# Value products of twelve heads in groups of four, sixteen places for transposed probabilities, one compressed transpose per four heads, and an end in token halves, in a two-layer decoder trunk

## The chip, the cores and the metric

The kernel runs on one core of one Trainium2 chip. The metric is the device time of one execution in microseconds (us). Three runs of the kernel before gave 577.61, 577.78 and 578.94 us, so the median is 577.78 us. The engines are named PE (TensorE, matrix products), PEld (its weight loads), DVE (VectorE), ACT (ScalarE), POOL (GpSimd) and SP (SyncE, which issues most transfers).

## The reference, cut to what matters

The trunk has two layers for 256 tokens of width 1024. Layer 0 is a recurrent block (gates, short convolution, scan) with a squared-ReLU MLP. Layer 1 is sparse attention with the same kind of MLP. A final norm ends it. With 256 tokens, a window of 512 and four selected blocks out of four, the selected and the window branch both see all earlier keys.

```python
x = x + _rglru_mixer(_rmsnorm(x, norm_mix[0]), ...);  x = x + _sq_relu_mlp(_rmsnorm(x, norm_ffn[0]), ...)
x = x + _nsa_mixer(_rmsnorm(x, norm_mix[1]), ...);    x = x + _sq_relu_mlp(_rmsnorm(x, norm_ffn[1]), ...)
return _rmsnorm(x, norm_final)
# in the attention, 16 heads in 4 groups that share keys and values:
o = g[..., 0:1] * o_c + g[..., 1:2] * o_s + g[..., 2:3] * o_w   # compressed, selected, window
```

The compressed branch has 15 keys: windows of 32 tokens at a stride of 16, each put through a small MLP. o_c, o_s and o_w are softmax(scores) times values, in each branch.

## The kernel before

All activations lie transposed: channels on the 128 partitions, 256 tokens along the free dimension, in 8 chunks. A weight comes in pieces of 128x1024 (load from L254), and ACT or DVE splits it into a high and a low part (L268, L277, or L316, L313 in the planned sections). mm3 (L307 to L310) makes each product of three matmuls of 128x256: high by high, high by low, low by high.

Two sections, the recurrent block (from 0 to about 62 us) and the attention (about 270 to 400 us), are written as lists of tasks with engine, length, due time and keys that they read or write. The class Plan turns such a list into one fixed order for every engine: it adds a random number up to SHIFT = 1.5 to each due time, from a seed (SEEDS = (11, 19), one for each section), lists, improves six times, and emits. Between and behind these sections run the two MLPs (function mlp), in an order written out by hand.

In the attention the steps that matter here are:
- hidden and vc_out make the 15 compressed values of each group. vc_out copies them to hv, multiplies by w2raw in four products of 64 columns (L944) and spreads them into bd, whose rows 64 to 127 are set to zero by POOL (L947 is the spreading).
- compressed(a) makes the compressed scores of four heads in bank 7, eleven steps on DVE and ACT make probabilities of them (cq: 128 query tokens by two token halves x 4 heads x 16 keys), two transposes (L1052), one for each token half, put them in bank 7, and ACT copies them (L1054) to pc: 64 partitions, 256 tokens.
- scores(s), rescale(s), transposes(s), for head s of 16: the scores of both other branches (L1075, L1076), the softmax (L1082, L1085), its scaling (L1104, L1105), and six transposes (L1116) with two copies into pT (L316). pT has 8 places of 128x384, two to a head.
- pv(j), j from 0 to 7, for two heads: the value products (L1127) into bank 7, two at a time for the two halves of the output partitions. A pair over pc and bd with 256 columns comes first, then for each branch a pair with 256 and a pair with 128 columns. All are float32, which is two matmul instructions each, so pv has 20. Then ACT or DVE copies the bank to oh (L316) and DVE makes the rest ol (L313).
- qchunk, kchunk and out_t: the projections before and behind, which fill PE between heads.

In the last MLP, m = 7 ends with: add to the residual (L508), square (L473), sums of squares over the partitions (L500), root (L1215) and reciprocal, spreading over the partitions (L505), six multiplications (L1220), and a transfer out of each (L1221).

Of the kernel before, what the change touches and what calls it, by code (L numbers as in the profile page):

```python
# [12 lines left out]
F32 = mybir.dt.float32  # L13
# [21 lines left out]
SEEDS, ROUNDS, SHIFT = (11, 19), 6, 1.5  # L35
# [184 lines left out]
def trunk_kernel(ctx: ExitStack, tc: tile.TileContext, x_in, vec_in, const_in, w2_in, wts, out):  # L220
# [524 lines left out]
    def mlp(layer, epilogue, first, late=None):  # L745
        with ExitStack() as ph:
            up = ph.enter_context(tc.tile_pool(name="up%d" % layer, bufs=1, side="right"))
            tmp = ph.enter_context(tc.tile_pool(name="mtmp%d" % layer, bufs=2))
            uhl = [up.tile([P, 2 * S], F32R, name="uhl", tag="uhl", bufs=NF) for _ in range(NF)]
# [24 lines left out]
            for m in range(8):  # L774
                z = next(zrot)[:, :S]
                for j in range(4):
                    if j == 3 and late and m == 7:
                        late()
                    wh, wl = get("dn%d" % layer, m * 4 + j)
                    for k in range(8):  # L780
                        w, i = slice(k * P, (k + 1) * P), j * 8 + k
                        mm3(z, wh[:, w], wl[:, w], uh[i], ul[i], i == 0, i == NF - 1)
                    if j == 3:
                        residual(z, m)
                        epilogue(m)
                    tick()
# [8 lines left out]
    with ExitStack() as ph:  # L795
# [9 lines left out]
        bd = at.tile([P, 4, 4, 64], F32, name="bd")  # L805
# [13 lines left out]
        pTt = at.tile([P, 8, 3 * P], F32, name="pT")  # L819
        pT = [pTt[:, i] for i in range(8)]  # L820
        w1 = many([P, 1024], F32, "w1", 2)
        pcs = many([P, S], F32, "pc", 2)
        for i in range(2):
            o = offs[-1] + (4 + i) * P * 1024
            add("sp", 1.5, lambda e, i=i, o=o: e.dma_start(w1[i], wts[o:o + P * 1024].rearrange("(p n) -> p n", p=P)),
                w=[("w1", i), "loads"], t=-12, lag=2.0)
        add("pool", 1.74, lambda e: e.memset(kl.bitcast(F32), 0.0), w=["kl"], t=-9)
        add("pool", 0.15, lambda e: e.memset(kc.bitcast(F32), 0.0), w=["kc0"], t=-9)
        add("pool", 0.9, lambda e: e.memset(bd[64:], 0.0), w=["bd0"], t=-8)
        for i in range(2):  # L830
            add("pool", 0.3, lambda e, i=i: e.memset(pcs[i][64:], 0.0), w=[("pc0", i)], t=-8)
# [52 lines left out]
        hid = pre.tile([P, 4, NCP], F32, name="hid")  # L884
        hv = pre.tile([P, 4, 2, 2, NCP], F32, name="hv")[64:]
        hvs = hid[64:]
        add("pool", 0.15, lambda e: e.memset(hid, 0.0), w=["hid"], t=-5)
# [19 lines left out]
        def hidden(b, t):  # L907
# [3 lines left out]
            for q_ in range(4):  # L911
# [4 lines left out]
                add("pe", 0.86, run, r=[("w1", i) for i in range(2)] + keys + zpt, w=[("ps", b)], t=t + 0.9 * q_)  # L916
# [4 lines left out]
                r=[("ps", b), "cb", "tab"], w=["hid"], t=t)  # L921

        def kc_out(t):
            o = zview("kco", 6, lambda x: x[:, :4 * NCP])
            add("pe", 0.3, lambda e: e.matmul(o(), w2raw[:64], hid[:64].rearrange("p g n -> p (g n)"), start=True, stop=True),
                r=["hid"], w=[("ps", 6)], t=t)
# [8 lines left out]
        def vc_out(t):  # L935
            for g in range(4):
                dst = hv[:, g // 2 * 2:g // 2 * 2 + 2, :, g % 2].rearrange("p a b n -> p (a b) n")
                add([("act", 0.2, 0.0), ("dve", 0.15, 0.0)], copy(dst, hvs[:, g, None, :].to_broadcast([64, 4, NCP])),
                    r=["hid"], w=[("hv", g)], t=t)
            o = zview("vco", 7, lambda x: x[:64, :4 * 64].rearrange("p (a e) -> p a e", a=4))  # L940
# [4 lines left out]
            add("pe", 0.9, run, r=[("hv", g) for g in range(4)], w=[("ps", 7)], t=t)  # L945
            for a in range(4):
                add("dve", 0.34, lambda e, a=a: e.tensor_tensor(  # L947
                    bd[:64, a], o()[:, a, None, :].to_broadcast([64, 4, 64]),
                    cst[:64, C_BM:C_BM + 4, None].to_broadcast([64, 4, 64]), op=OP.mult), r=[("ps", 7)], w=[("bd", a)], t=t)
# [47 lines left out]
        css, cs2, cmx = many([P, 4, 2, NCP], F32, "cs", 2), many([P, 2, 4, NCP], F32, "cq", 2), many([P, 8], F32, "cm", 2)  # L997
# [4 lines left out]
        def compressed(a, t, dt):  # L1002
# [39 lines left out]
            for i, (d, fn, r, w) in enumerate(steps):  # L1042
                if d == "act":
                    add("act", 0.2, fn, r=r, w=w, t=t + dt * i)
                else:
                    add("dve", d, fn, r=r, w=w, t=t + dt * i)
            t += dt * len(steps)
            ct_ = zview(("ct", a), 7, lambda x: x[:64, :S])

            def tr(e):  # L1050
                for qc in range(2):
                    e.transpose(ct_()[:, qc * P:(qc + 1) * P], sq_[:, qc].rearrange("p j n -> p (j n)"), identf)  # L1052
            add("pe", 0.22, tr, r=[qk], w=b7, t=t)
            add("act", 0.26, lambda e: e.copy(pc[:64], ct_()), r=b7, w=[pk], t=t)  # L1054
# [53 lines left out]
        def transposes(s, t):  # L1108
            pt = pts[s % NPT]
            for b in range(2):  # L1110
# [7 lines left out]
                i = s // 2 % 2 * 4 + s % 2 * 2 + b  # L1118
                add([("act", 0.38, 0.0), ("dve", 0.47, 0.2)], lambda e, tp=tp, i=i: copy(pT[i], tp())(e), r=bk, w=[("pT", i)], t=t + 0.3)

        def pv(j, t):
            p, a, n0 = j // 4, j // 2, j % 2 * 4
            bk = [("ps", 7)]
            o = zview(("o", j), 7, lambda x: x[:, :S])

            def run(e):
                two = lambda c0, w, y, **k: [e.matmul(o()[own_(hf), c0:], w(hf), y(hf), **k) for hf in range(2)]  # L1127
                two(0, lambda hf: bd[:, a, j % 2 * 2 + hf], lambda hf: pcs[a % 2], start=True, stop=False)
                for b in range(2):
                    y = lambda hf: pT[n0 + 2 * hf + b]  # L1130
                    two(0, lambda hf: vv[:, 0, b, 2 * p + hf], lambda hf: y(hf)[:, :S], start=False, stop=False)
                    two(P, lambda hf: vv[:, 1, b, 2 * p + hf], lambda hf: y(hf)[:, S:], start=False, stop=b == 1)
# [197 lines left out]
```

## Time and profile before

| | us |
|---|---|
| median of three runs | 577.78 |
| the profiled execution, its own time | 578.3 |
| its span in the trace | 576.5 |
| PE busy in the span | 564.8 |
| PE busy from 302 to 382 us (heads) | 79.81 of 80 |
| DVE busy there | 75.78 of 80 |
| from the start of the last addition to the residual to the end of the span | 9.4 |

The span is what the trace covers; the profiled execution's own time has 1.8 us more around it. "Busy" counts an engine as working while an instruction is under way. PE's instructions overlap: one of 256 columns is shown with 0.28 us and the next starts 0.11 us later. So what an instruction costs in a full stream is read from start to start. The page's TensorE clock is full in all but the last of 40 slices.

### The profile page before, as it was taken

What the parts mean: (1) busy time and instruction counts of PE and PEld (TensorE: products, weight loads), DVE (VectorE), ACT (ScalarE), POOL (GpSimd) and SP (SyncE); (2) the same over time, 40 slices, a digit from 0 to 9 for tenths busy, and PEclk for the clock granted to TensorE, in tenths of its full rate; (3) what the DMA queues carried; (4) which work ended last, traced back from release to release, by engine and by line L of the source; (5) the groups of instructions that cost most, each with busy time, mean ns of one, the idle gap of its engine ahead of it and who ended that gap; (6) DMA issues with size and microseconds to landing.
All of it is one profiled execution on the core that took longest, in us unless ns stands there. A gap on an engine that the chain in (4) does not pass through costs nothing.

```text
span 576.5 us, 12291 instructions
## 1 busy us (share of the span) xinstructions
PE 564.8 (98%) x4866; PEld 552.6 (96%) x4866; DVE 411.8 (71%) x841; ACT 338.6 (59%) x656; POOL 47.0 (8%) x60
## 2 busy tenths in 40 slices
PE   8999999999999999999999999999999999999994
PEld 7999999999999999999999888989999999999994
DVE  6899999766775664665759999978876775553522
ACT  7699585865663533444457989865766564443400
POOL 1210000000000211312000000000000000222310
PEclk9999999999999999999999999999999999999998
DMA  8934566766666566466573243243666667467302
GB/s 291 395 115 147 187 221 195 211 211 185 195 204 221 161 209 215 155 207 241 186 261 121 70 124 127 100 118 137 190 204 194 189 197 237 155 207 223 113 1 73
DMA packets 32378, 103.66 MB, mean 180 GB/s; under 512 B 4017, under 2 KB 7217, under 8 KB 32321
## 3 DMA queue, kind: packets, MB, share of 16 engines
q1 hardware_dynamic: 31712, 102.29, 54.9%
q8 instruction: 38, 0.62, 0.4%
q10 hardware_dynamic: 576, 0.53, 0.3%
q14 instruction: 20, 0.16, 0.1%
q0 software_dynamic: 32, 0.07, 0.0%
HBM read 99.23 MB, written 1.05 MB: 174 GB/s over the span
## 4 chain that ended last, share of the span: by engine, by line
PE 87%; DVE 7%; DMA 2%; ACT 1%; issue 1%; SPq 0%; DVEq 0%
PE bank L308 26%; PE bank L310 25%; PE bank L309 25%; PE bank L1127 3%; PE bank L1116 2%; DVE wlo L313 2%; DVE xb L645 2%; DMA raw<-in_dram 1%; PE bank L1075 1%; DMA xt<-in_dram 1%; PE bank L1076 1%; PE bank L965 1%; PE bank L966 1%; PE bank L967 1%; PE bank L915 1%
## 5 line engine op out<-in xcount | busy, mean ns | idle before, releaser
L308 PE MATMUL bank<-hhl,whi 128*128 128x256 f32 x768 | 214.3, 279 | 1.1 <-DVE whi L316 0.6
L310 PE MATMUL bank<-hhl,wlo 128*128 128x256 f32 x768 | 212.6, 277 | 0.8 <-DVE wlo L313 0.8
L309 PE MATMUL bank<-hhl,whi 128*128 128x256 f32 x768 | 212.6, 277 | 0.1
L308 PEld LDWEIGHTS bank<-hhl,whi 128*128 128x128 f32 x768 | 144.2, 188 | 1.9 <-ACT x L562 0.8
L310 PEld LDWEIGHTS bank<-hhl,wlo 128*128 128x128 f32 x768 | 144.2, 188 | 1.2 <-DVE wlo L313 1.2
L277 DVE TENSOR_TENSOR wlo<-raw,whi 128x1024 fp32r<-128x1024 f32 x115 | 143.6, 1269 | 2.3 <-ACT whi L268 2.3
L309 PEld LDWEIGHTS bank<-hhl,whi 128*128 128x128 f32 x768 | 144.2, 188 | 0.6 <-DVE hhl L558 0.3
L308 PE MATMUL bank<-uhl,whi 128*128 128x256 f32 x512 | 141.5, 276 | 0.0
L309 PE MATMUL bank<-uhl,whi 128*128 128x256 f32 x512 | 141.4, 276 | 0.0
L310 PE MATMUL bank<-uhl,wlo 128*128 128x256 f32 x512 | 141.4, 276 | 0.0
L268 ACT CAST whi<-raw 128x1024 fp32r<-128x1024 f32 x116 | 118.0, 1039 | 23.1 <-issue 18.8
L308 PEld LDWEIGHTS bank<-uhl,whi 128*128 128x128 f32 x512 | 96.1, 188 | 0.0
L310 PEld LDWEIGHTS bank<-uhl,wlo 128*128 128x128 f32 x512 | 96.1, 188 | 0.0
L309 PEld LDWEIGHTS bank<-uhl,whi 128*128 128x128 f32 x512 | 96.1, 188 | 0.0
L313 DVE TENSOR_TENSOR wlo<-raw,whi 128x1024 fp32r<-128x1024 f32 (+2 forms) x74 | 79.2, 1091 | 7.4 <-ACT whi L316 7.3
L508 DVE TENSOR_TENSOR xt<-xt,bank 128x256 f32<-128x256 f32 x40 | 16.1, 417 | 85.9 <-PE bank L310 85.8
L316 ACT CAST whi<-raw 128x1024 fp32r<-128x1024 f32 (+2 forms) x65 | 62.1, 969 | 21.9 <-DMA raw<-in_dram 7.5
L760 ACT ACTIVATE u<-t 128x256 f32<-128x256 f32 x64 | 26.7, 417 | 59.0 <-DVE t L755 59.0
L755 DVE SCALAR_TENSOR_TENSOR t<-bank,rstd 128x256 f32<-128x256 f32 x64 | 26.9, 423 | 40.8 <-PE bank L310 40.8
L1210 ACT ACTIVATE xg<-xt,vec 128x256 f32<-128x256 f32 x8 | 4.1, 511 | 48.0 <-DVE xt L508 48.0
L1085 ACT ACTIVATE pt<-pt,mx 128x128 f32<-128x128 f32 (+1 forms) x64 | 28.6, 449 | 4.2 <-DVE mx L1082 3.9
L478 POOL TENSOR_TENSOR acc<-xt 128x256 f32<-128x256 f32 x2 | 2.9, 1464 | 344.2 <-DVE xt L508 189.3
(191 smaller groups left out, 746.1 us busy)
## 6 DMA issues: line engine op xcount, KB each, us to landing
raw<-in_dram SPq DMA_DIRECT2D x173, 512.0 KB, 4.2
raw<-in_dram SPq DMA_DIRECT2D x4, 560.0 KB, 5.0
gw<-in_dram SPq DMA_DIRECT2D x4, 512.0 KB, 8.8
raw<-in_dram SPq DMA_DIRECT2D x6, 256.0 KB, 5.9
xt<-in_dram SPq DMA_DIRECT2D x4, 256.0 KB, 5.7
w<-in_dram SPq DMA_DIRECT2D x2, 512.0 KB, 6.0
kh<-kh SPq DMA_DIRECT2D x8, 64.0 KB, 2.7
kl<-tl SPq DMA_DIRECT2D x8, 64.0 KB, 2.9
```

Of the source, the lines that this page charges most:

```text
L268: (act.copy if eng is None else eng.tensor_copy)(hi_t[i % NSPL][:, :n], raw_t[i % NRAW][:, :n])
L277: (eng or dve).tensor_tensor(lo[:, :n], raw_t[i % NRAW][:, :n], hi[:, :n].bitcast(F32), op=OP.subtract)
L308: pe.matmul(ps, wh, xh, start=start, stop=False)
L309: pe.matmul(ps, wh, xl, start=False, stop=False)
L310: pe.matmul(ps, wl, xh, start=False, stop=stop)
L313: return lambda e: e.tensor_tensor(o, a, h.bitcast(F32), op=OP.subtract)
L316: return lambda e: (e.copy if e is act else e.tensor_copy)(o, a)
L508: dve.tensor_tensor(xt[:, m], xt[:, m], z, op=OP.add)
L755: dve.scalar_tensor_tensor(t, z, 0.0, rs, op0=OP.max, op1=OP.mult)
L760: act.activation(u, t, AF.Square)
L1085: add("act", (0.39, 0.49)[qc], lambda e, row=row, j=j: e.activation(row, row, AF.Exp, bias=mx[:, j:j + 1], scale=-1.0, accum_out=sm[:, j:j ...
L1127: two = lambda c0, w, y, **k: [e.matmul(o()[own_(hf), c0:], w(hf), y(hf), **k) for hf in range(2)]
```

## The change

Five things change.
- The value products are made for js = (0, 1), (2, 3), (4, 5), (6,), (7,): three times a run of 48 instructions for four heads, into all 512 columns of bank 7, and twice a run of 24 for two heads. The due time is that of the last member. One copy and one remainder follow each run, over 512 or 256 columns.
- pT has 16 places. The two pieces w1 of hidden lie in places 8 to 13 in place of tiles of their own, with keys that keep them apart.
- The probabilities of the compressed branch are transposed once for four heads, both token halves together (128 partitions, 128 tokens). bd holds masked values for both halves, and the pair over pc and bd becomes two pairs of 128 columns. vc_out has two products with 128 columns of weights in place of four with 64, and two wider spreadings in place of four; the settings to zero go.
- hid, hv, and the scores and probabilities of the compressed branch lie in the tiles sq0 and sq1, which the norms use, with keys for that.
- The end: PE adds the old residual of the last chunk into its bank at the start of m = 7 (two matmuls with the identity). ACT then squares the bank directly, by token halves; sums, root, reciprocal and spreading are made for each half in banks of their own, then once more into banks 0 and 1 for a copy in SBUF, and five multiplications and transfers follow, the first two of 3 chunks by half the tokens.

The seeds of both planned sections are others, too: (3, 0) for (11, 19).

```diff
-SEEDS, ROUNDS, SHIFT = (11, 19), 6, 1.5
+SEEDS, ROUNDS, SHIFT = (3, 0), 6, 1.5
...
+                if last and m == 6:
+                    act.copy(ir, ident)
+                    act.copy(xh, xt[:, 7])
+                    diff(xl, xt[:, 7], xh)(dve)
+                if seeded:
+                    pe.matmul(z, ir, xh, start=True, stop=False)
+                    pe.matmul(z, ir, xl, start=False, stop=False)
...
-        pTt = at.tile([P, 8, 3 * P], F32, name="pT")
-        w1 = many([P, 1024], F32, "w1", 2)
-        pcs = many([P, S], F32, "pc", 2)
+        NPT_ = 16
+        pTt = at.tile([P, NPT_ * 3 * P], F32, name="pT")
+        w1 = [pTt[:, 8 * 3 * P + i * 1024:8 * 3 * P + (i + 1) * 1024] for i in range(2)]
+        w1k = [("pT", i) for i in range(8, 14)]
+        pcs = many([P, P], F32, "pc", 2)
...
-                for a in range(4):
-                    e.matmul(o()[:, a], hv[:, a].rearrange("p b f n -> p (b f n)"), w2raw[64:, :64], start=True, stop=True)
+                for p in range(2):
+                    e.matmul(o()[:, p], hv[:, p].rearrange("p b f n -> p (b f n)"), w2raw[64:, :64], start=True, stop=True)
...
-                for qc in range(2):
-                    e.transpose(ct_()[:, qc * P:(qc + 1) * P], sq_[:, qc].rearrange("p j n -> p (j n)"), identf)
-            add("act", 0.26, lambda e: e.copy(pc[:64], ct_()), r=b7, w=[pk], t=t)
+            add("pe", 0.11, lambda e: e.transpose(ct_(), sq_.rearrange("p q j n -> p (q j n)"), identf), r=[qk, ("sq", 1)], w=b7, t=t)
+            add([("act", 0.3, 0.0), ("dve", 0.2, 0.15)], lambda e: copy(pc, ct_())(e), r=b7, w=[pk], t=t)
...
+                    for qc in range(2):
+                        two(tok[qc], lambda hf: bd[:, p, qc * 4 + j % 2 * 2 + hf], lambda hf: pcs[a % 2], start=qc == 0,
+                            stop=False)
...
-        for j in range(8):
-            events.append((T0 + (2 * j + 3.4) * T, 1, lambda j=j: pv(j, T0 + (2 * j + 3.4) * T)))
+        for js in ((0, 1), (2, 3), (4, 5), (6,), (7,)):
+            t = T0 + (2 * js[-1] + 3.4) * T
+            events.append((t, 1, lambda js=js, t=t: pv(js, t)))
...
+    def finish(z):
+        for i in range(2):
+            act.activation(sqh[i], z[:, tok[i]], AF.Square)
+        for i in range(2):
+            pe.matmul(sts[i][:, :1], sqh[i], ones, start=False, stop=True)
+        dve.tensor_scalar(xg[:, 7], z, vec[:, V_GL + 7:V_GL + 8], None, op0=OP.mult)
+        for i in range(2):
+            act.activation(rcs[i], sts[i][:, :1], AF.Sqrt, bias=epst, scale=1.0 / D)
+        for i in range(2):
+            dve.reciprocal(rcs[i], rcs[i])
+            pe.matmul(sts[i][:, S:S + P], rcs[i].to_broadcast([P, P]), ident, start=True, stop=True)
+        for i in range(2):
+            pe.matmul(dup[i][:, :P], rcs[i].to_broadcast([P, P]), ident, start=True, stop=True)
...
+    for i in range(2):
+        act.copy(rs[:, tok[i]], dup[i][:, :P])
+    for n, (a, b, i) in enumerate(((0, 3, 0), (0, 3, 1), (3, 5, 2), (5, 7, 2), (7, 8, 2))):
+        c = tok[i] if i < 2 else slice(0, S)
+        scaled(a, b, c, sts[i][:, S:S + P] if i < 2 else rs)
+        (nc.scalar if n % 2 else nc.sync).dma_start(out[:, a:b, c], xg[:, a:b, c])
```

## Rows read from the trace of the kernel before

**Rows 1.** From the page: the span, and busy time, share of the span and instructions of each engine.

```profile
span 576.5 us, 12291 instructions
PE 564.8 (98%) x4866; PEld 552.6 (96%) x4866; DVE 411.8 (71%) x841; ACT 338.6 (59%) x656; POOL 47.0 (8%) x60
```

**Rows 2.** The waits of PE over the whole span: for whom it waited, in total, how often, and the longest. The waits of the end are left out.

```profile
PE bank L310 <- DVE wlo L313: 0.8, 2, 0.7
PE bank L308 <- DVE whi L316: 0.6, 1, 0.6
PE bank L308 <- ACT hhl L556: 0.5, 1, 0.5
PE bank L1075 <- DMA sa<-tl: 0.2, 1, 0.2
```

**Rows 3.** Busy time by stretch: the recurrent section, the first MLP, the heads of the attention, the last MLP. Columns: stretch, its length, busy time and (instructions) of PE, PEld, DVE, ACT and POOL, the granted TensorE clock as a share of 2.4 GHz, the DMA share, GB/s.

```profile
0.00:65.00 65.00, 61.61 (x456) 58.91 (x457) 58.12 (x122) 50.68 (x96) 8.27 (x20) 1.00 0.62 219
65.00:180.00 115.00, 115.00 (x1014) 115.00 (x1013) 91.72 (x148) 76.14 (x132) 0.00 (x0) 1.00 0.65 207
302.00:382.00 80.00, 79.81 (x675) 71.81 (x675) 75.78 (x315) 66.38 (x208) 0.00 (x0) 1.00 0.37 112
480.00:570.00 90.00, 88.41 (x776) 87.92 (x774) 39.62 (x40) 30.40 (x37) 18.76 (x13) 1.00 0.44 140
```

**Rows 4.** The order of PE's instructions among the heads (timeline, PE alone): start, time under way, line, operation, operands, how many in a row. First a pair of compressed transposes, then a value product between transposes, then one in front of a projection.

```profile
329.57 0.38 PE L1052 MATMUL bank<-cst,cq 128*64 128x128 f32 x2
329.71 0.37 PE L308 MATMUL bank<-hhl,whi 128*128 128x256 f32 x1
...
330.50 0.49 PE L1116 MATMUL bank<-cst,pt 128*128 128x128 f32 x3
330.92 0.65 PE L1127 MATMUL bank<-pc,bd 128*64 128x256 f32 x4
331.41 1.47 PE L1127 MATMUL bank<-pT,vv 128*64 128x256 f32 x16
332.81 0.55 PE L1116 MATMUL bank<-cst,pt 128*128 128x128 f32 x3
...
334.46 0.65 PE L1127 MATMUL bank<-pc,bd 128*64 128x256 f32 x4
334.94 1.47 PE L1127 MATMUL bank<-pT,vv 128*64 128x256 f32 x16
336.34 0.39 PE L308 MATMUL bank<-hhl,whi 128*128 128x256 f32 x1
336.56 0.28 PE L309 MATMUL bank<-hhl,whi 128*128 128x256 f32 x1
```

**Rows 5.** The same view in the recurrent section: 56 float32 matmuls of 128x256 with weights of 128 columns, with nothing between, and what follows.

```profile
31.93 12.25 PE L665 MATMUL bank<-xb,gw 128*128 128x256 f32 x56
43.83 0.47 PE L308 MATMUL bank<-hhl,whi 128*128 128x256 f32 x1
```

**Rows 6.** The same view at the products of vc_out (64 columns of weights, 64 columns moved) and at the early sums of squares (128 columns of weights, one column moved), each with what follows.

```profile
286.81 0.65 PE L944 MATMUL bank<-w2raw,hv 64*64 64x64 f32 x8
287.38 0.41 PE L965 MATMUL bank<-whi,hhl 128*128 128x304 f32 x1
...
563.63 0.50 PE L500 MATMUL bank<-ones,acc 128*128 128x1 f32 x4
564.00 0.37 PE L308 MATMUL bank<-uhl,whi 128*128 128x256 f32 x1
```

**Rows 7.** Groups of instructions by line, operation and shape: count, busy time, mean ns of one, idle time before them.

```profile
L316 ACT COPY pT<-bank 128x384 f32<-128x384 f32 x30 | 13.6, 474 | 2.5 <-PE bank L1116 2.2
L316 ACT CAST oh<-bank 128x256 fp32r<-128x256 f32 x8 | 3.0, 372 | 2.6 <-PE bank L1127 2.5
L1031 ACT ACTIVATE cs<-cs 128x128 f32<-128x128 f32 x4 | 1.3, 313 | 0.4 <-DVE cs L1030 0.2
L313 DVE TENSOR_TENSOR ol<-bank,oh 128x256 fp32r<-128x256 f32 x8 | 3.3, 414 | 2.2 <-ACT oh L316 2.2
L316 DVE COPY pT<-bank 128x384 f32<-128x384 f32 x2 | 1.1, 547 | 0.0
```

**Rows 8.** The end in order of time (timeline, all engines). The first row is PE's last matmul of the last MLP.

```profile
566.82 0.28 PE L310 MATMUL bank<-uhl,wlo 128*128 128x256 f32 x1
567.13 0.42 DVE L508 TENSOR_TENSOR xt<-xt,bank 128x256 f32<-128x256 f32 x1 [11.04 <-PE bank L310]
...
567.66 0.42 DVE L473 TENSOR_TENSOR sq<-xt 128x256 f32<-128x256 f32 x1
...
568.14 0.61 PE L500 MATMUL bank<-ones,sq 128*128 128x1 f32 x4 [1.04 <-DVE sq L473]
568.78 0.26 ACT L1215 ACTIVATE rcol<-bank,epst 128x2 f32<-128x2 f32 x1 [0.68 <-PE bank L500]
569.08 0.17 DVE L1216 RECIPROCAL rcol<-rcol 128x2 f32<-128x2 f32 x1 [0.99 <-ACT rcol L1215]
...
569.29 0.71 PE L505 MATMUL bank<-cst,rcol 128*128 128x128 f32 x4 [0.55 <-DVE rcol L1216]
570.04 2.61 DVE L1220 TENSOR_TENSOR xg<-xg,bank 128x256 f32<-128x256 f32 x6 [0.80 <-PE bank L505]
```

More of the change, by code (lines that the diff above doesn't have):

```diff
@@ L743, in trunk_kernel, with mlp @@
         sec.emit(SEEDS[0])
-    def mlp(layer, epilogue, first, late=None):
+    def mlp(layer, epilogue, first, late=None, last=None):
         with ExitStack() as ph:
@@ L748, in mlp @@
             tmp = ph.enter_context(tc.tile_pool(name="mtmp%d" % layer, bufs=2))
+            if last:
+                xh, xl, ir = (tmp.tile([P, n], F32R, name=a, bufs=1) for a, n in (("xh", S), ("xl", S), ("ir", P)))
             uhl = [up.tile([P, 2 * S], F32R, name="uhl", tag="uhl", bufs=NF) for _ in range(NF)]
@@ L775, in mlp @@
                 z = next(zrot)[:, :S]
+                seeded = last is not None and m == 7
+                if last and m == 6:
[5 more added lines that the diff above has]
+                    pe.matmul(z, ir, xl, start=False, stop=False)
                 for j in range(4):
-                    if j == 3 and late and m == 7:
+                    if j == 3 and seeded:
                         late()
@@ L781, in mlp @@
                         w, i = slice(k * P, (k + 1) * P), j * 8 + k
-                        mm3(z, wh[:, w], wl[:, w], uh[i], ul[i], i == 0, i == NF - 1)
-                    if j == 3:
+                        mm3(z, wh[:, w], wl[:, w], uh[i], ul[i], i == 0 and not seeded, i == NF - 1)
+                    if j == 3 and seeded:
+                        last(z)
+                    elif j == 3:
                         residual(z, m)
@@ L804, in trunk_kernel @@
         vv = at.tile([P, 2, 2, 4, 64], F32, name="vv")
-        bd = at.tile([P, 4, 4, 64], F32, name="bd")
+        bd = at.tile([P, 2, 8, 64], F32, name="bd")
         gts = at.tile([P, 2, NH, 3], F32, name="gts")
@@ L915, in run @@
                             e.matmul(hp()[own_(i)], w1[i][:, l * 64:(l + 1) * 64], zfs[i][:, :, l], start=l == 0, stop=l == 15)
-                add("pe", 0.86, run, r=[("w1", i) for i in range(2)] + keys + zpt, w=[("ps", b)], t=t + 0.9 * q_)
+                add("pe", 0.86, run, r=[("w1", i) for i in range(2)] + keys + zpt + w1k, w=[("ps", b)], t=t + 0.9 * q_)
             t += 3.6
@@ L996, in trunk_kernel @@
         mxs, sms = many([P, 4], F32, "mx", 4), many([P, 4], F32, "sm", 4)
-        css, cs2, cmx = many([P, 4, 2, NCP], F32, "cs", 2), many([P, 2, 4, NCP], F32, "cq", 2), many([P, 8], F32, "cm", 2)
+        cmx = many([P, 8], F32, "cm", 2)
+        css = [ahf[:, i * P:(i + 1) * P].rearrange("p (j q n) -> p j q n", j=4, q=2) for i in range(2)]
+        cs2 = [alf[:, i * P:(i + 1) * P].rearrange("p (q j n) -> p q j n", q=2, j=4) for i in range(2)]
         heads = [(p, c, hf) for p in range(2) for c in range(4) for hf in range(2)]
@@ L1126, in run @@
             def run(e):
[L1127 to L1132, printed above, removed]
@@ new lines, in pv @@
+            ps = sorted({j // 4 for j in js})
+            add("pe", 1.54 * n + 0.35, run, r=[("pT", j % 4 * 4 % NPT_ + i) for j in js for i in range(4)] + [("bd", p) for p in ps] +
+                [("pc", j // 2 % 2) for j in js] + [("v", h, b) for h in range(2) for b in range(2)], w=bk, t=t)
+            ok, lk = ([(x, j) for j in js] for x in ("oh", "ol"))
+            add([("act", 0.1 + 0.24 * n, 0.0), ("dve", 0.07 + 0.27 * n, 0.2)], lambda e: copy(oht[:, cols], o())(e), r=bk, w=ok,
+                t=t + 1.9 * n)
```

88 lines of the change are left out of this document (46 added, 42 removed).

## The prediction

> **What bounds the kernel now.** I read the page first: PE is busy for 564.8 of 576.5 us, DVE for 411.8 [rows 1]. A busy PE may still be slow, so the waits come next: outside the end PE waits for 2.1 us in all, 1.9 of it for split weights and activations in the recurrent section, 0.2 for a moved query among the heads [rows 2]. Then the stretches: in the MLPs PE and PEld are both full, among the heads PE is busy for 79.81 of 80 us and DVE for 75.78 [rows 3]. Last the order of PE's instructions, since only distances from start to start tell what one costs [rows 4]. So the kernel is a chain of PE work from about 62 to 567 us, and behind it an end of 9.4 us in which the engines wait for each other [rows 8]. An edit between 270 and 400 us counts by the PE time that it takes out; what it saves on DVE and ACT counts only where PE waits for them. An edit of the end counts by its chain.
>
> **Value products.** Their own work first. The float32 matmuls of the recurrent section give a price without gaps: 56 in 43.83 - 31.93 = 11.90 us, 0.2125 us for 256 columns (the first starts beside the tail of its forerunner; I take 0.215) [rows 5]. A pair of pv runs its two halves beside each other at that price: two pairs over bd take 334.94 - 334.46 = 0.48 us, where 2 x 0.215 = 0.43 would do, and the rest (four instruction pairs of 256 and four of 128 columns, 4 x 0.215 + 4 x 0.1075 = 1.29) takes 336.34 - 334.94 = 1.40 [rows 4]. So a run pays about 0.05 at its start and 0.11 at its end. Ahead of it, three transposes take 330.92 - 330.50 = 0.42, where three at 0.11 are 0.33: another 0.09. A projection right behind pays 0.22 for its first matmul, not 0.12: 0.10 more, where no transposes stand between [rows 4]. One run thus costs 0.25 to 0.35 us beyond its work, every time that PE changes between 128-wide and 64-wide output tiles. Eight runs become five, so three such costs go: 0.75 to 1.05, and I take 0.9. The work itself stays: a pair of 256 columns becomes two of 128, whose price per column is the same inside vv (1.40 us holds both widths [rows 4]). The extra eight instructions per two heads could cost something if 128 columns didn't cover a weight load; those over vv do cover it, so I put it at nothing, with 0.2 in all as the upper end.
>
> **Compressed transposes.** Two of them take 0.14 us from the first to the projection behind, which then pays 0.2 for its first matmul [rows 4]; three transposes of full width at 0.11 show the price of one. Four of the eight go: 4 x 0.11 = 0.44 us, between 0.3 (if part of it hides in the change of the stream) and 0.44. I take 0.43.
>
> **vc_out.** The eight instructions of 64 weight columns take 287.38 - 286.81 = 0.57 us with their exit, 0.06 to 0.07 each. The early sums of squares move one column each, but load 128 columns of weights, and four take 564.00 - 563.63 = 0.37 us, 0.09 to 0.11 each [rows 6]. The new products are four instructions with 128 columns of weights: nearest to the second row, so 4 x 0.11 = 0.44 against 8 x 0.06 = 0.48, and I take no gain; the end of the range is 0.2.
> Counting instructions alone would make this half of 0.48, a gain of 0.24 us. The Trainium skill speaks against that ("TensorE: Matmul & The Clock Gate", section "LDWEIGHTS (loading the stationary operand)"): a weight load takes as long as it has columns, whatever the depth of the contraction. By that rule half as many loads of twice the width gain nothing, and the sums of squares, at about 0.1 us with one column moved, agree.
>
> **DVE, ACT, POOL.** Two copies of oh at 0.372 and two remainders at 0.414 become one of each over 512 columns [rows 7]; with the fixed part saved, 0.1 us each, three times on both engines. The zero settings on POOL go, and ACT copies 128 columns to pc in place of 256. All of this lies beside a PE that is busy, and costs or gives nothing while it stays so. The 16 places let transposes run ahead of the value products by twice as many heads; the old 8 caused no wait that PE shows [rows 2], so this is room for the grouping, not a gain. A run for four heads is one long piece of 3.7 us in PE's fixed order and waits for eight places, for pc and for bank 7. Behind it in PE's queue stand scores and projections. Due times of the last members are as before, so what out_t reads comes at the same place. w1 in places 8 to 13 is read before the first head; head 4 is the first to write there, so SP's loads and POOL's memsets get no new wait on the path. The keys on sq0 and sq1 join work that lies a stage apart.
>
> **The end.** PE first pays two more matmuls for the old residual, 0.23 us at 0.1134 each (115.00 us by 1014 in the first MLP [rows 3]); the three preparations, about 0.4 us each [rows 7], stand in ACT's and DVE's queues one chunk, some 11 us, earlier [rows 8], where ACT has 30.40 us of work in 90 and DVE 39.62 [rows 3]; PE waits for none of it. Let A be the moment at which the old addition began, 567.13, just after PE's last matmul [rows 8]. Before: addition, square, sums, root, reciprocal and spreading bring the first multiplication to 570.04, A + 2.91, and the last ends at 572.65, A + 5.52 [rows 8]. After, for the first half: square 0.31 (128 columns on ACT, rows 7), 0.06 to PE, two sums 0.38 (0.61 for four less two steps of 0.11), 0.03 and root 0.26, 0.04 and reciprocal 0.17, 0.04 and spreading 0.49 (0.71 for four less two steps), 0.04: A + 1.82. The second half follows 0.2 to 0.3 behind. DVE makes two products of 384 columns, at 2.61 us per 2048 [rows 8] 0.98 us, to A + 2.80. The other three wait for rs: second spreading to A + 2.1, two more to A + 2.5, two ACT copies of about 0.3: A + 3.1. They have 1280 columns, 1.63 us: A + 4.73. That is 0.8 sooner than A + 5.52, less 0.23 for the seed matmuls: 0.55 to 0.65. If ACT's steps overlap as DVE's do it is 0.9; if the transfers of half rows, which the trace has none of, land later, it is 0.2. I take 0.65. From the last multiplication to the span's end I keep 576.5 - 572.65 = 3.9 us.
>
> **The new seeds.** They deal all orders anew, in the recurrent section too, where nothing else changes. What that does isn't in the trace. Bounds: PE's waits there are 1.9 us, of which 0.8 are for split weights [rows 2], so the gain ends at about 0.8 there and 0.2 among the heads; a poor order can as well show those waits twice, 1.9 us more. The middle that I take is nothing.
>
> **The sum.** 0.9 + 0.43 + 0 + 0.65 = 1.98 us. The profiled execution, 578.3 us with a span of 576.5, becomes 576.3; it stands 0.5 above the median of the runs. The median of 577.78 becomes 575.8. A measurement of this kernel can tell about 0.3% from no change, which is 1.7 us: 576.05 and 579.5 are the bounds, and the forecast lies barely beyond the first.
>
> **Rivals.**
> - *PE time among the heads isn't the limit.* Taken-out work then turns into waits, and only the end's 0.65 comes: 577.1 us. For it: DVE has 4.2 us of idle in 80, and PEld is busy for 71.81 only [rows 3]. Against it: the distances from start to start are those of a full stream [rows 4, 5].
> The Trainium skill ("Trainium Kernel Development and Optimization", section "Performance Expectations") warns that matmul busy time is a bad measure and weight loads are the better one. By that rule 8.2 us of the 80 could be waits; but pairs beside each other and 512-column scores need fewer loads for the same time, so I give it little.
> - *DVE becomes the bound: slower.* Each of the 32 copies to pT is made by ACT or DVE as the plan sees fit, 30 by ACT at 0.474 and 2 by DVE at 0.547 [rows 7]. The new order may give DVE more. Its idle of 4.2 us, less 1.3 by which PE's work shrinks, plus 0.4 of saved remainders and copies, is 3.3: up to six copies moved are free, and from the seventh on each costs 0.55 us of the stage. Thirteen moved (7.1 us) make the stage 3.8 longer than forecast: 579.6 us.
> - *The new order also sheds old waits:* 0.8 in the recurrent section and 0.2 to 0.4 among the heads: 574.7 us.
> - *The grouping doesn't do what it says:* if the change of tile widths is paid at each two heads inside a run too, 0.9 goes: 576.7 us.
>
> **How the numbers follow.** Forecast 0.50, own range 574.8 to 576.9; DVE bound 0.12; PE not the limit 0.15; waits shed 0.17; cost inside runs 0.06. Faster than 576.05: 0.35 of the forecast's 0.50 and the shed waits, 0.52. Slower: 0.12. The rest, 0.36, is no change that can be told. The range runs from 574.0, the shed waits with the end's 0.9, to 578.5, which takes in PE not being the limit and a recurrent section with 1.4 us more waits; it leaves out the DVE bound and the tails.
>
> **What would show it.** Value products in five runs, with 48 instructions in about 3.6 us and no pause in the middle; four compressed transposes; PE still without waits among the heads, which then end some 1.3 us sooner; the first multiplication 1.8 us after PE's last matmul, the last at 4.7. I am wrong if PE waits for DVE or for copies among the heads, if the stretch up to 62 us changes by more than 0.5 us, or if the last transfer lands later than 3.9 us after its multiplication.

## The result and the profile after

Six runs of the changed kernel gave 574.90 to 575.71 us, median 575.4; six of the kernel before in the same session gave 577.55 to 578.94, median 578.15. The ratio is 0.994, with an interval of 0.9929 to 0.9952: faster by 0.6%, or 2.75 us, where 1.98 were forecast. The profiled execution took 574.91 us.

First the page, then PE's waits over the whole span, the end included, then the heads (columns as in [rows 3]):

```profile
span 573.1 us, 12338 instructions
PE 564.2 (98%) x4896; PEld 555.4 (97%) x4896; DVE 410.7 (72%) x835; ACT 339.8 (59%) x660; POOL 44.7 (8%) x57
```

```profile
PE bank L550 <- POOL warm L547: 1.3, 1, 1.3
PE bank L308 <- DVE whi L316: 1.1, 1, 1.1
PE bank L1245 <- ACT sqh L1243: 0.4, 1, 0.4
PE bank L1251 <- DVE rc L1250: 0.3, 1, 0.3
```

```profile
302.00:382.00 80.00, 80.00 (x719) 74.28 (x718) 75.64 (x312) 65.12 (x204) 0.00 (x0) 1.00 0.38 110
```

PE has 30 instructions more than before [rows 1]: 32 more value products, two seed matmuls and four more for the spreading at the end, less four compressed transposes and four products of vc_out. The first of the waits, ahead of the warm matmuls (products on zeros at the very start), stands in the trace of before with the same 1.3 us; [rows 2] and the 2.1 us of the prediction leave it out. Among the heads PE waits for nothing any more (the 0.2 us of [rows 2] is gone), and DVE stands at 75.64 us of 80, for 75.78 [rows 3].

PE's busy time over the whole span falls by 0.6 us only. In the stretch of the attention, cut as in the table below, it falls by 1.96 (before, then after):

```profile
263.25:479.30 216.05, 215.86 (x1888) 206.82 (x1887) 173.87 (x483) 149.41 (x355) 4.46 (x14) 1.00 0.52 162
262.91:476.81 213.90, 213.90 (x1911) 207.58 (x1910) 173.29 (x478) 148.60 (x352) 2.99 (x11) 1.00 0.53 164
```

Elsewhere it grows: by 0.67 us ahead of it (172.80 to 173.47), where the clock rose later, by 0.25 for the seed matmuls, by 0.45 in the end. So a sum over the span hides what the change gave.

PE's timeline at the first run for four heads, then at vc_out:

```profile
329.39 0.28 PE L310 MATMUL bank<-hhl,wlo 128*128 128x256 f32 x1
329.51 0.27 PE L1065 MATMUL bank<-cst,sq 128*128 128x128 f32 x1
329.53 0.37 PE L308 MATMUL bank<-hhl,whi 128*128 128x256 f32 x1
329.74 0.28 PE L309 MATMUL bank<-hhl,whi 128*128 128x256 f32 x1
...
330.21 0.28 PE L310 MATMUL bank<-hhl,wlo 128*128 128x256 f32 x1
330.42 0.66 PE L1141 MATMUL bank<-pc,bd 128*64 128x128 f32 x8
330.91 1.47 PE L1141 MATMUL bank<-pT,vv 128*64 128x256 f32 x16
332.21 0.61 PE L1141 MATMUL bank<-pc,bd 128*64 128x128 f32 x8
332.64 1.47 PE L1141 MATMUL bank<-pT,vv 128*64 128x256 f32 x16
334.05 0.87 PE L1128 MATMUL bank<-cst,pt 128*128 128x128 f32 x6
```

```profile
286.30 0.65 PE L958 MATMUL bank<-w2raw,sq 64*128 64x64 f32 x4
286.87 0.41 PE L979 MATMUL bank<-whi,hhl 128*128 128x304 f32 x1
```

The run of 48 takes 334.05 - 330.42 = 3.63 us and has no pause where its second member begins. One compressed transpose and the projection matmul behind it take 329.74 - 329.51 = 0.23 us. The four products of vc_out take 0.57 us, as the eight did [rows 6].

The end in order of time, after PE's last matmul:

```profile
564.58 0.28 PE L310 MATMUL bank<-uhl,wlo 128*128 128x256 f32 x1
564.90 0.45 ACT L1243 ACTIVATE sqh<-bank 128x128 f32<-128x128 f32 x2 [10.74 <-PE bank L310]
...
565.23 0.61 PE L1245 MATMUL bank<-ones,sqh 128*128 128x1 f32 x4 [0.37 <-ACT sqh L1243]
...
565.65 0.48 ACT L1248 ACTIVATE rc<-bank,epst 128x1 f32<-128x1 f32 x2 [0.31 <-PE bank L1245]
565.94 0.39 DVE L1250 RECIPROCAL rc<-rc 128x1 f32<-128x1 f32 x2
...
566.16 0.71 PE L1251 MATMUL bank<-cst,rc 128*128 128x128 f32 x4 [0.33 <-DVE rc L1250]
...
566.68 1.02 DVE L1259 TENSOR_TENSOR xg<-xg,bank 128x384 f32<-128x384 f32 x2 [0.35 <-PE bank L1251]
...
567.13 0.49 ACT L1262 COPY rstd<-bank 128x128 f32<-128x128 f32 x2 [1.00 <-PE bank L1253]
...
567.65 1.63 DVE L1259 TENSOR_TENSOR xg<-xg,rstd 128x512 f32<-128x512 f32 x3
```

The first multiplication starts 566.68 - 564.90 = 1.78 us after ACT's first square, the first step behind PE's last matmul; the last ends at 567.65 + 1.63 = 569.28, 4.38 after it; before it was 5.52 [rows 8].

**Where the time went.** I cut each trace at four instructions of PE that every kernel has: the first down matmul of the first MLP, its last, the first down matmul of the last MLP, its last. Most of the experiments are read from this table, too (us, one profiled execution each; "clock" is the moment from which the granted clock stays at 2.4 GHz, until it falls in the end, at 568.2 to 571.7 us). From the first to the last down matmul of the first MLP every kernel takes 87.06 us; that column is left out.

| kernel | to MLP 1's down half | attention and up half | last down half | end | span | clock |
|---|---|---|---|---|---|---|
| before, seeds (11, 19) | 176.19 | 216.05 | 87.52 | 9.70 | 576.5 | 4.8 |
| e1, before with (3, 0) | 175.63 | 216.08 | 87.52 | 9.71 | 576.0 | 5.0 |
| e10, before with (3, 1) | 175.88 | 215.60 | 87.52 | 9.72 | 575.8 | 4.3 |
| e8, before with grouping | 176.79 | 215.15 | 87.52 | 9.70 | 576.2 | 10.6 |
| e2, after, eight runs | 176.32 | 214.52 | 87.77 | 8.55 | 574.2 | 10.9 |
| e9, the same, seeds (11, 19) | 176.72 | 214.58 | 87.77 | 8.55 | 574.7 | 10.9 |
| **after**, seeds (3, 0) | 175.85 | 213.90 | 87.77 | 8.55 | 573.1 | 9.6 |
| e5, after with (11, 19) | 175.57 | 214.38 | 87.77 | 8.55 | 573.3 | 5.4 |
| e6, after, 8 places | 175.90 | 214.04 | 87.77 | 8.56 | 573.3 | 5.0 |
| e4, after, transposes twice | 176.23 | 214.15 | 87.77 | 8.54 | 573.7 | 10.5 |
| e2b, after, runs broken | 176.22 | 215.34 | 87.77 | 8.55 | 574.9 | 10.4 |
| e3, after, old end | 176.81 | 213.93 | 87.52 | 9.87 | 575.2 | 11.8 |
| e7, after, 22 warm matmuls | 175.85 | 214.44 | 87.77 | 8.54 | 573.7 | 7.4 |
| e11, after, four runs | 175.62 | 213.57 | 87.77 | 8.54 | 572.6 | 9.4 |

From before to after the span loses 3.4 us: 0.34 in the first stretch, 2.15 in the attention, 1.15 in the end, less 0.25 for the two seed matmuls. The two profiled executions lie 0.2 above and 0.5 below their medians, which is the rest to 2.75.
How far a number of this table can be trusted it shows itself: after, e3 and e7 have one and the same order in the attention and take 213.90, 213.93 and 214.44 there. Half a microsecond between two executions is therefore nothing. (0.37 of it lies in the matmuls of hidden, 4.11 us in e7 for 3.74 in after.)

A second cut helps. PE's time in the attention stretch, from the start of each instruction to the next one's, added up by kind (us):

| kind | before | e1 | e10 | e8 | e2 | e9 | after | e5 | e6 | e2b | e11 |
|---|---|---|---|---|---|---|---|---|---|---|---|
| value products | 15.06 | 15.06 | 15.06 | 14.61 | 15.10 | 15.10 | 14.65 | 14.65 | 14.65 | 15.11 | 14.50 |
| compressed transposes | 0.62 | 0.77 | 0.62 | 0.54 | 0.19 | 0.18 | 0.37 | 0.31 | 0.11 | 0.37 | 0.37 |
| projections, scores, transposes | 191.31 | 191.33 | 190.62 | 190.98 | 190.28 | 190.49 | 189.96 | 190.66 | 190.10 | 189.95 | 189.92 |
| everything else | 9.05 | 8.92 | 9.30 | 9.01 | 8.95 | 8.80 | 8.92 | 8.77 | 9.19 | 9.91 | 8.77 |

### The profile page after: what moved, and what is told of

It is laid out like the page before. It is cut to its first block, busy times and chain, and to the rows that moved or that the text cites. A ratio compares the mean times of both kernels' runs of the same rounds, so it can differ in the third digit from the quotient of the medians.

```text
span 573.1 us, 12338 instructions
## 1 busy us (share of the span) xinstructions
PE 564.2 (98%) x4896; PEld 555.4 (97%) x4896; DVE 410.7 (72%) x835; ACT 339.8 (59%) x660; POOL 44.7 (8%) x57
## 4 chain that ended last, share of the span: by engine, by line
PE 98%; DMA 1%; DVE 1%; ACT 0%; DVEq 0%; issue 0%
PE bank L308 28%; PE bank L310 28%; PE bank L309 28%; PE bank L1141 3%; PE bank L665 2%; PE bank L1128 2%; PE bank L1087 1%; PE bank L1088 1%; PE bank L979 1%; PE bank L980 1%; PE bank L981 1%; DMA vec<-in_dram 1%; PE bank L929 1%; PE bank L1031 1%; DVE xg L1259 0%; PE bank L505 0%
## 5 line engine op out<-in xcount | busy, mean ns | idle before, releaser
L308 PE MATMUL bank<-hhl,whi 128*128 128x256 f32 x768 | 214.7, 280 | 1.1 <-DVE whi L316 1.1
L764 DVE TENSOR_TENSOR uhl<-u,uhl 128x256 fp32r<-128x256 f32 x64 | 26.6, 416 | 2.9 <-ACT uhl L763 2.9
```

Source lines behind the costliest of these rows:

```text
L308: pe.matmul(ps, wh, xh, start=start, stop=False)
L764: later(lambda: dve.tensor_tensor(ul[m], u, uh[m].bitcast(F32), op=OP.subtract))
```

## The experiments

My theory was the prediction's: PE's time is the limit, and what is taken out of its stream comes out of the span. The rivals were that the gain comes from the new seeds (an order that happens to be good, or that sheds old waits), that it comes from the 16 places, that the width change is paid inside a run all the same, and that the end alone gains.

**The seeds alone** (e1, e10 on the kernel before; e5 on the kernel after).

```diff
-SEEDS, ROUNDS, SHIFT = (11, 19), 6, 1.5
+SEEDS, ROUNDS, SHIFT = (3, 0), 6, 1.5        # e1;  e10: (3, 1);  e5: (3, 0) back to (11, 19)
```

> The kernel before with the new seeds alone (3 and 0 for 11 and 19). If PE time and the end explain the result, the seeds are worth what the stretch up to 62 us lost, 0.3 us, and at most 0.4 us among the heads (the one wait there): 577.4 us beside 578.15, and the last MLP starts 0.3 to 0.7 us sooner than in the kernel before. If the new order is the cause of most of the attention's 2.1 us, this kernel gets 1.5 us or more of them: its last MLP starts at least 1.5 us sooner and the time is 576.5 or less.

> The kernel before with seeds 3 and 1: a third order of its attention, which took 216.05 us with seed 19 and 216.08 with seed 0. If orders at equal work differ by some tenths, 215.7 to 216.5. If the kernel before had been held back by two unlucky orders, 215.2 or less.

> The changed kernel with the seeds of the kernel before (11 and 19). The new seeds alone gave the old kernel 0.56 us up to the first product of the first MLP's second half and 0.0 in the attention. If the work taken out is what counts, this kernel's attention takes 214.7 us (216.05 less the 0.9 and 0.43 of the prediction), 0.8 more than with seed 0, and its time is 576.4 us. If seed 0 is what gives the attention its 2.1 us together with the new tasks, the attention takes 215.5 us or more and the time is 577.2 or more. If any order does as well, 213.9 and 575.9.

e1: median 578.06 of 12 runs against 578.4, ratio 0.9993 (0.9984 to 1.0003); the attention takes 216.08 for 216.05. e10, one run: 577.57 us, 215.60. e5: 575.93 against 578.3, ratio 0.996 (0.9945 to 0.9974), which overlaps the interval of after. e10's attention came just below the 215.7 to 216.5 that were expected, e5's 214.38 between the 213.9 and the 214.7. On the old kernel the seeds give nothing that can be told (the interval leaves at most 0.9 us), and on the new one at most what the intervals leave open. In e5 PE meets one new wait, for the probabilities of a compressed branch:

```profile
PE bank L1065 <- DVE sq L1053: 0.3, 1, 0.3
```

**Eight runs for two heads** (e2 with the new seeds, e9 with the old).

```diff
-        for js in ((0, 1), (2, 3), (4, 5), (6,), (7,)):
+        for js in ((0,), (1,), (2,), (3,), (4,), (5,), (6,), (7,)):
```

> The changed kernel with eight value products for two heads each, each at the due time that it had in the kernel before. If every run pays for a change of the width of PE's output tiles, three more runs cost 0.75 to 1.05 us of PE time: 576.3 us beside 575.4. If the grouping gives nothing, 575.4, within 0.3. The plan has other tasks and so another order, which may move it by some tenths; the count of changes between streams of instructions is read beside it.

> The changed kernel with eight value products and the seeds of before: all of the change in the attention but the grouping, in the order of another seed than the earlier run of this kind, which took 214.52 us. If what is left of the change is only the 0.43 us of the compressed transposes, the attention takes 215.6 us. If it is worth 1.5 us whatever the order, 214.5. In between, the rest of the 1.5 was the luck of one order.

e2: 575.94 against 578.4, ratio 0.9957 (0.9943 to 0.9972); e9, one run: 576.46. So with the grouping undone more than half of the gain stays, and the attention still takes 214.52 and 214.58 in place of 216.05. That is the 1.5 us of e9's second case: what the change does in the attention beside the grouping is worth more than the 0.43 us of the prediction. e2's 575.94 lies between its two cases. Against the grouped kernel of the same seeds the stretch is 0.62 longer (new seeds) and 0.20 (old seeds, where e5 has the wait above). These differences also hold a new order. The value products themselves don't: 15.10 us in both, 14.65 in both grouped ones, so three removed runs give 0.45 inside the products, 0.15 each.

**Broken runs** (e2b): the order of after, but between the members of a run PE makes one transpose of 128 columns into the part of the bank that the second member then overwrites. PE changes its tile width twice more in each of three runs.

```diff
                 for j in js:
+                    if j > js[0]:
+                        e.transpose(o()[:, S:S + P], identf, identf)
```

> The changed kernel in its own order, with one more transpose of 128 output partitions between the two members of each of the three groups (its result is overwritten). The transpose itself costs 0.11 us each, 0.33 in all. If a change of the tile width costs 0.25 to 0.35 us, each group takes 3.63 + 0.11 + 0.3 = 4.0 us and the last MLP starts 1.1 to 1.4 us later: 576.6 us. If the change of width is free and the cost of a run lies in what stands around it, the groups take 3.74 us and the last MLP starts 0.33 us later: 575.7 us.

576.42 against 578.4, ratio 0.9968 (0.9956 to 0.998). PE's timeline at the same run:

```profile
331.00 0.66 PE L1143 MATMUL bank<-pc,bd 128*64 128x128 f32 x8
331.49 1.47 PE L1143 MATMUL bank<-pT,vv 128*64 128x256 f32 x16
332.89 0.33 PE L1141 MATMUL bank<-cst 128*128 128x128 f32 x1
333.15 0.66 PE L1143 MATMUL bank<-pc,bd 128*64 128x128 f32 x8
333.64 1.47 PE L1143 MATMUL bank<-pT,vv 128*64 128x256 f32 x16
335.04 0.87 PE L1128 MATMUL bank<-cst,pt 128*128 128x128 f32 x6
```

335.04 - 331.00 = 4.04 us for 3.63, and the other two runs of four heads give 4.04 for 3.63 as well. Of the 0.41 the transpose itself is 0.11; 0.30 is the change of width there and back. Three times 0.41 is 1.23 of the 1.44 us by which the stretch grew (the other 0.2 is in the matmuls of hidden, which the edit doesn't touch).

**The grouping alone** (e8), on the kernel before, with its 8 places and its seeds.

```diff
-        def pv(j, t):
+        def pv(js, t):
...
+                for j in js:
+                    p, a, n0, c0 = j // 4, j // 2, j % 2 * 4, (j - js[0]) * S
...
-        for j in range(8):
-            events.append((T0 + (2 * j + 3.4) * T, 1, lambda j=j: pv(j, T0 + (2 * j + 3.4) * T)))
+        for js in ((0, 1), (2, 3), (4, 5), (6,), (7,)):
+            t = T0 + (2 * js[-1] + 3.4) * T
+            events.append((t, 1, lambda js=js, t=t: pv(js, t)))
```

> The kernel before with the grouping of its value products alone (five runs in place of eight, 8 places, its own transposes, end and seeds). If a removed run is worth 0.25 to 0.35 us wherever it stands, the attention takes 215.0 to 215.3 us, against 216.05, and the time falls by 0.7 to 1.05, to about 577.4 beside 578.3. If the grouping only pays together with the new transposes and memory, the attention stays within 0.4 of 216.05 and the time within 0.4 of before. If the groups cause waits with 8 places, the attention is longer than 216.05.

577.26 of 11 runs against 578.56, ratio 0.9978 (0.9969 to 0.9987). The attention takes 215.15 for 216.05, or for 215.91 as the mean of three orders without grouping (215.60 to 216.08): 0.8 to 0.9 us, although PE met a wait of 0.5 us in this order:

```profile
PE bank L925 <- ACT hid L919: 0.5, 1, 0.5
```

**A fourth group** (e11), which the kernel doesn't have.

```diff
-        for js in ((0, 1), (2, 3), (4, 5), (6,), (7,)):
+        for js in ((0, 1), (2, 3), (4, 5), (6, 7)):
```

> The changed kernel with the last two value products in one run, too: four runs of four heads. By the price of a run, PE saves another 0.2 to 0.37 us: attention 213.6, time 575.1. Against it: the first half of the last run now waits for heads 14 and 15, and behind it stand the last projections, which need its output; if PE has nothing else left then, it waits, and the attention takes 214.2 or more.

574.87 against 578.56, ratio 0.9946 (0.9933 to 0.9959), which can't be told from after's. In the trace the value products fall by another 0.15 to 14.50 and the stretch by 0.33 to 213.57, without a wait. Of the 0.33, 0.04 is in the neighbours and 0.15 in everything else, in hidden again; so the trace shows 0.2 for the fourth run, the lower end of the 0.2 to 0.37 expected.

```profile
376.33 0.66 PE L1141 MATMUL bank<-pc,bd 128*64 128x128 f32 x8
376.82 1.47 PE L1141 MATMUL bank<-pT,vv 128*64 128x256 f32 x16
378.12 0.61 PE L1141 MATMUL bank<-pc,bd 128*64 128x128 f32 x8
378.56 1.47 PE L1141 MATMUL bank<-pT,vv 128*64 128x256 f32 x16
```

**Each compressed transpose twice** (e4), four in all, into the same place.

```diff
-            add("pe", 0.11, lambda e: e.transpose(ct_(), ...), ...)
+            add("pe", 0.11, lambda e: [e.transpose(ct_(), ...) for _ in range(2)], ...)
```

> The changed kernel in its own order, with each of the four compressed transposes made twice. If a transpose of full width costs 0.11 us on PE's path, the attention takes 0.44 us more, 214.35 against 213.9. If its weight load and its stream hide beside the projections around it, less than 0.2 more.

One run: 575.55 us. In the same order the attention grows from 213.90 to 214.15, and the compressed transposes from 0.37 to 0.70: 0.08 us for each transpose, where 0.11 was counted. The stretch lies between the two cases expected.

**Eight places** (e6): w1 in tiles of its own, pT with 8 places.

```diff
-        NPT_ = 16
+        NPT_ = 8
...
-        w1 = [pTt[:, 8 * 3 * P + i * 1024:8 * 3 * P + (i + 1) * 1024] for i in range(2)]
-        w1k = [("pT", i) for i in range(8, 14)]
+        w1 = many([P, 1024], F32, "w1", 2)
+        w1k = []
```

> The changed kernel with 8 places for transposed probabilities as before (w1 in tiles of its own again), the groups of four heads kept. A group then takes all 8 places, and the transposes of the next four heads wait until its products are done. If the 16 places are what makes the grouping possible without waits, PE waits for copies or transposes among the heads and the attention takes 1 us or more longer than 213.9, 215 to 217 us. If the plan finds other work for that time, the attention takes 214.2 at most, and the 16 places are worth nothing.

One run: 575.13 us; attention 214.04 for 213.90, no wait of PE there. The 16 places give nothing that shows.

**The old end** (e3): the last MLP and what follows as before.

```diff
-                seeded = last is not None and m == 7
+                seeded = False
...
-    mlp(1, to_final, up1, early_sums, finish)
+    st = bank(6)
+    mlp(1, to_final, up1, lambda: square_sums(st, acc, True, False))
+    square_sums(st, sqs[1], False, True)
...
```

> The changed kernel with the end of the kernel before: no seed matmuls, the addition, the square and the whole chain for all 256 tokens, six transfers. By the two traces the new end is worth 1.13 us from PE's last matmul on, less 0.24 for the seed matmuls: 0.9 us, so 576.3 us beside 575.4, with the last MLP starting at the same time. If the half-token transfers give part of it back, or the seed matmuls cost more than they show, it is nearer to 575.6.

576.32 against 578.4, ratio 0.9964 (0.9951 to 0.9977). The end is 9.87 - 8.55 = 1.32 us longer, the last down half 0.25 shorter: that makes 1.07 us for the new end, while the attention takes 213.93 as in after. But 0.17 of it is not the edit's. The old end takes 9.70 to 9.72 us in the four other kernels that have it. In this execution the clock fell during the spreading, at 568.2 us (in the second row the clock is the number ahead of the last two), and its matmuls took 0.88 us for 0.71 [rows 8]:

```profile
567.79 0.88 PE L505 MATMUL bank<-cst,rcol 128*128 128x128 f32 x4 [0.55 <-DVE rcol L1237]
567.50:569.00 1.50, 0.88 (x4) 0.58 (x4) 0.46 (x2) 0.04 (x1) 0.00 (x0) 0.73 0.00 0
```

Without it the new end is worth 0.90 us, as between before and after. The first stretch, which the edit doesn't touch, is 0.96 longer; I come to that in the last section.

**More warm matmuls** (e7), made because the clock rose at different moments.

```diff
-WARM = 16
+WARM = 22
```

> The changed kernel with 22 matmuls on zeros in front of the first product in place of 16. In the profiles so far PE ends the 16 at about 5 us, is idle until 5.6 to 6.5, and the granted clock goes from 1.2 to 2.4 GHz at 4.8 to 10.9 us, once with a fall in between; the stretch up to 176 us is up to 1.2 us longer where that is late. If the idle gap before the first product is what delays the clock, six more matmuls bridge it, the clock rises once, by 8.5 us, the stretch takes 175.6 us, and the median falls by 0.3 to 0.5 us to about 575.0. If the moment is set otherwise, the first product starts no sooner, the rise scatters as before, and the median stays within 0.2 of 575.4.

575.21 of 6 runs (574.47 to 576.35) against 578.3, ratio 0.9945 (0.993 to 0.996). The clock rose at 7.4 us in place of 9.6, the first stretch is the same 175.85, and the time can't be told from after's. So the idle time was bridged and the clock rose before 8.5 us, as the first case had it, but the gain that this case forecast didn't come.

## Why the prediction was right

575.8 us was forecast and 575.4 measured; the likeliest case is the one that came, with 2.75 us for a sum of 1.98. By its steps:

- **What bounds the kernel.** PE's stream, as said. PE is busy for 80.00 of 80 us among the heads, instructions taken out shorten the stretch and instructions put in lengthen it (e2b, e4). The rival that PE's time is not the limit has fallen: with the old end (e3) the gain would have gone, and e3 is still 0.36% faster than before. The rival that DVE becomes the bound didn't occur: ACT still makes 30 of the 32 copies to pT, DVE's 75.64 us are within 0.14 of before's.
- **Value products: the size holds, and the mechanism is shown.** 0.25 to 0.35 us for a run, 0.9 for three. e2b puts one change back into an otherwise equal order and pays 0.30 beyond the transpose, three times alike; e8 gives 0.8 to 0.9 on the old kernel. Of the 0.30, 0.15 lies inside the products (15.10 to 14.65 for three runs), and the rest in the neighbours: the last projection ahead of a run takes 330.42 - 330.21 = 0.21 us in place of 0.11. The rival that the change is paid inside a run has fallen with 3.63 us. The Trainium skill ("TensorEngine Tiling (Array Packing)", section "Tiling Modes") says that a change of tiling mode, not just of the tile, drains TensorE. The broken runs agree, at 0.30 us for a change there and back. The 32 added instructions of half the width cost 15.10 - 15.06 = 0.04 (the prediction speaks of eight more per two heads; it is four).
- **Compressed transposes: right.** In the kernel before, two transposes and the projection matmul behind them took 329.91 - 329.57 = 0.34 us [rows 4]; one and its follower take 0.23 now, 0.11 less, at three of the four places. At the fourth, at 349.23 us, the transposes behind it start 0.2 late; in e2 all four save the 0.11. By kind the sums fall from 0.62 to 0.77 down to 0.11 to 0.37, and e4 puts the price at 0.08. So 0.3 to 0.4 for 0.43. The row of before:

```profile
329.91 0.28 PE L309 MATMUL bank<-hhl,whi 128*128 128x256 f32 x1
```

- **vc_out: nothing, as said.** 0.57 us for four products with 128 columns of weights and for eight with 64.
- **The end: the mechanism right, the size at the upper edge.** The first multiplication came 1.78 us after the first step for 1.82. The last ended at 4.38 for 4.73, because rs was ready at 567.13 + 0.49 = 567.62, 2.72 after, for 3.1. ACT's two copies began at 2.23 for 2.5, while PE was still spreading, and took 0.49 together, where each was put at 0.3. From the last multiplication to the end of the span there are 573.1 - 569.28 = 3.8 us for 3.9; the two transfers of half the tokens landed in 2.3 and 2.6 us, those of before in 1.9 to 2.7. With 0.25 for the seed matmuls the net is 0.90, for 0.65 within 0.2 to 0.9. This is the term that was mis-sized; the prediction's own steps give 0.79 - 0.23 = 0.56, and 0.65 was the upper end of what it made of them. The new end leaves out the addition and halves the data, and no run takes these apart.
- **The seeds: nothing that can be told, as said** (e1). The 16 places: nothing (e6).
- **Shed waits, the other likely rival, in part.** PE's wait of 0.2 us among the heads is gone. By kind, projections, scores and transposes, which the change leaves as they are, fall from 191.1 (mean of before, e1 and e10) to 190.4 in the ungrouped kernels e2 and e9, and to 190.0 in after. The last step holds the neighbours of the removed runs. The first, 0.7 us, is the part of the gain that no term of mine names. Part of it is pauses at single places, longer than the waits of PE tell. In before the wait of 0.2 us costs 308.39 - 307.81 = 0.58 us from start to start, where the same matmul takes 0.23 at other heads:

```profile
307.81 0.40 PE L1076 MATMUL bank<-kl,sb 128*128 128x512 f32 x1
308.39 0.36 PE L1075 MATMUL bank<-kh,sa 128*128 128x256 f32 x1 [0.19 <-DMA sa<-tl]
```

In e1 three transposes ahead of a compressed pair take 352.40 - 351.82 = 0.58 us and three behind it 353.13 - 352.65 = 0.48, for 0.33 each. Such pauses come and go with the order: e10 has none of this size and takes 190.6, and e5, the whole change with the old seeds, has new ones (its wait of 0.3 costs 328.88 - 328.17 = 0.71 for 0.23) and takes 190.7. Three orders of the kernel before lie 0.7 apart. So part of the unnamed 0.7 us is the luck of the orders dealt. Whether the change sheds pauses by itself, by the compressed branch's shorter chain, its single transposes or the sharing of sq0 and sq1, no run takes apart, and the cause stays open.

In the sum: grouping 0.9 for 0.9, compressed transposes 0.3 to 0.4 for 0.43, end 0.9 for 0.65, an unnamed 0.7 for nothing. That is 2.8 to 2.9 us, for 2.75 in the medians and 3.4 between the two profiled executions, whose first stretches differ by 0.34, where the change gives only another order. The named terms are right to within 0.25. The 0.7 the forecast put at nothing, and the rival of shed waits put the heads' share at 0.2 to 0.4. (By its own terms the lower bound of the range is 574.7 - 0.25 = 574.45, not 574.0; nothing hangs on it.)

## What to carry to other kernels

Where PE is full, read the distances from start to start at the joints between kinds of matmul: every change of the output tile's width cost about 0.15 us here, so products of the narrow width belong together in long runs. In an end that is a chain of small steps over three engines and the transfers, leaving out the addition and halving the data, so that the first half's step runs beside the second's, gained 0.9 us net, which no busy time shows. Before a gain of half a microsecond is believed, look at what the same order takes in two executions, and at a piece of PE's stream whose instructions repeat exactly. A wait that a list shows with 0.2 us can cost more from start to start.

## What the runs showed of the hardware that was not expected

**The clock rises at a different moment in each execution.** All kernels but e7 make 16 warm matmuls that end at about 5 us; PE then idles for 0.6 to 1.4 us until the first weights are split. In the profile of before the granted clock was full from 4.8 us and stayed so up to the end. In that of after PE's first projections run at the lower level, 0.21 us apart (1.2 GHz), until 9.6 us, and then 0.12 apart:

```profile
9.10 0.41 PE L308 MATMUL bank<-hhl,whi 128*128 128x256 f32 x1
9.31 0.41 PE L309 MATMUL bank<-hhl,whi 128*128 128x256 f32 x1
9.52 0.33 PE L310 MATMUL bank<-hhl,wlo 128*128 128x256 f32 x1
9.69 0.28 PE L308 MATMUL bank<-hhl,whi 128*128 128x256 f32 x1
9.81 0.28 PE L309 MATMUL bank<-hhl,whi 128*128 128x256 f32 x1
```

In e3 it was full at first, fell to 0.50 at 8.4 us after PE had idled for 1.41 us ahead of its first projection, and rose again at 11.8. By stretch (columns as in [rows 3]; the clock is the number ahead of the last two):

```profile
8.50:11.80 3.30, 3.07 (x14) 2.78 (x14) 3.30 (x11) 3.30 (x11) 0.00 (x0) 0.50 1.01 370
11.90:15.00 3.10, 3.10 (x29) 3.10 (x29) 3.10 (x8) 2.92 (x8) 2.25 (x1) 1.00 0.83 293
```

In the five executions with a full clock by 5.4 us the first stretch takes 175.83 us on average (175.57 to 176.19), in the six where it came at 10.4 or later 176.52 (176.22 to 176.81). That is 0.7 us, a quarter of what the whole change gained. The seeds don't make it: PE's order in this stretch is one and the same in the ten executions with seed 3, which take 175.62 to 176.81, and in the four with seed 11, which take 175.57 to 176.79. But it is a correlation over 14 executions, and not a plain one: where the clock came at 7.4 to 9.6 us (e7, e11 and after) the stretch takes 175.62 to 175.85, no longer than with an early clock. And e7, which meant to move the clock, moved it by 2.2 us and gained nothing that can be told. Why the stretch differs between executions of one order stays open.
